# Sums of weights behind the low parts, another order of the first loads, and a shorter last 1/rms in a hybrid decoder

## The chip, the cores and the metric

The kernel runs on one core of one Trainium2 chip. The metric is the device time of one execution in microseconds (us). The core has five engines that each take their own queue of instructions in order: TensorE (PE, matrix products), VectorE (DVE), ScalarE (ACT), GpSimd (POOL) and SyncE (SP, which here issues the DMAs). They wait for one another through semaphores. PE's products land in PSUM, which has eight banks; the other engines read them from there.

## What is computed

A decoder of two layers on 512 tokens of 1024 features, float32. Each layer adds half of a SwiGLU network, then a mixer (gated linear attention in the first layer, stick-breaking attention in the second), then half of another network; an RMSNorm stands ahead of each and behind all:

```python
def rmsnorm(x, g):
    return x * lax.rsqrt(jnp.mean(x * x, axis=-1, keepdims=True) + EPS) * g

def swiglu(h, w_gate, w_up, w_down):          # 1024 -> 2816 -> 1024
    return (jax.nn.silu(h @ w_gate) * (h @ w_up)) @ w_down

for i in range(2):
    x = x + 0.5 * swiglu(rmsnorm(x, ffn1_norm[i]), ffn1_w_gate[i], ...)
    x = x + mixer_i(rmsnorm(x, mix_norm[i]))
    x = x + 0.5 * swiglu(rmsnorm(x, ffn2_norm[i]), ffn2_w_gate[i], ...)
return rmsnorm(x, final_norm)
```

## The kernel before, in words

The activations lie with features on the partitions: eight tiles of 128 features by 512 tokens (`x0` to `x7`). Weights come from memory in blocks of 1 MB (`raw`, gate and up, two buffers) and 512 KB (`rawd`, down, two buffers); SP issues these loads in its queue, and a load waits until the last reader of its buffer is done.

Full precision is had by splitting. ACT casts a block to a rounded high part (`wh`, line 126, in `Entry.split`), DVE subtracts it to get the low part (`wl`, line 127), and each product becomes three: high times high, low times high, high times low (`mm3`, line 68). The activations are split likewise (`nh`, `nl`; `hh`, `hl` by lines 788 and 789; `th`, `tl`).

The networks are computed in part by Strassen's scheme, with seven products of half blocks for eight. It needs sums and differences of the four quarters of a weight block: `s12` and `s34`, two DVE steps each, in `seven` at lines 677, 678, 683 and 684 (gate and up) and in `seven_down` at lines 353 to 361 (down). `Entry.view` (line 103) records these sums and `Entry.split` then cuts them like raw weights. `Feed.start` looks ahead: when a block's products begin, the next two entries are split, the next three viewed, the next five loaded. So a sum is recorded some blocks ahead of its product, at the point where its entry comes into view.

`seven` has two bodies. At the end of an up block stand these steps on what PE left in the banks: u3 from `ps_w` (line 736, ACT) and the sum with it (737, DVE); `ps_q` added into `o0` (740, DVE); the gate, a product of `o1` and `o0` each with the gate's part (707, DVE, in the shape `o<-o,o`); and the last quarter, `o1` from `ps_w` times the gate's part (707, DVE, in the shape `o<-ps_w,o`). Each reads a bank that a later product will use again: the banks go round in order of use. At three places in each network a down block follows at once, in `seven_down`: its first products are 12 into two new `ps_w` banks, 12 into two new `ps_q` banks (line 369), and then again 12 into the `ps_w` banks, which must first have been copied to `ps_z` by ACT (line 387). In the trace the tiles of `seven` are at line 694 and those of `seven_down` at 369.

The opening is written out by hand, with every instruction pinned in its order: `x` comes in halves of features, is turned by PE (line 1574), scaled by the norm's gain and split by ACT and DVE (1580, 1584), while squares for the norm are taken by ACT and DVE (1558, 1562); the first gate and up blocks are cut in halves (1544, 1546) and multiplied (1599). `keep` copies the turned tiles to `x0` to `x7` (1591, 1593).

At the end, `to_tokens` turns the activations back to tokens on partitions, and `last` (line 1458 and on) adds the last network's products to them in pieces, sums their squares (ACT, line 1471), takes 1/rms by `rstd_1` (495 to 506: a square root on ACT, a reciprocal and one Newton step on DVE), multiplies and writes out (1478 to 1481) by two DMAs on SP for each 128 tokens.

Of the kernel before, what the change touches and what calls it, by code (L numbers as in the profile page):

```python
# [10 lines left out]
F32 = mybir.dt.float32  # L11
# [21 lines left out]
def decoder(ctx: ExitStack, tc: tile.TileContext, a: dict, out: bass.AP):  # L33
    nc = tc.nc
# [59 lines left out]
    class Entry:  # L94
# [7 lines left out]

        def view(self):

            if self.views is None:
                self.views = [view(ch.load()) for ch, view, _, _ in self.units]
            return self.views

        def split(self):
            if self.W is None:  # L110
                self.W = []
                for r, (_, _, n, m) in zip(self.view(), self.units):
                    few = n * m < 1024
                    if few:

                        h = st["few"].tile([P, n * m + NEAR], F32R, tag="vh", bufs=1, name="wh")[:, NEAR:]
                        l = st["few"].tile([P, n * m + 64 - NEAR], F32R, tag="vl", bufs=1, name="wl")[:, : n * m]
                    else:
                        h, l = (
                            wp.tile([P, n * m + 64], F32R, tag="w" + t, bufs=4, name="w" + t)[  # L120
                                :, self.place : self.place + n * m
                            ]
                            for t in "hl"
                        )
                    h, l = (t.rearrange("p (n m) -> p n m", m=m) for t in (h, l))
                    st["cut"] = nc.scalar.copy(h, r).ins  # L126
                    nc.vector.tensor_tensor(out=l, in0=r, in1=h.bitcast(F32), op=ALU.subtract)  # L127
                    self.W.append((h, l))
                    if self.lead and len(self.W) == 1:


                        first = wp.tile([P, P], F32R, tag="w1", bufs=1, name="w1")
                        with tc.issue_after(st["cut"]):
                            nc.scalar.copy(first, r[:, 0, 0:P])
                        self.first = first
# [323 lines left out]
    st = {}  # L459
# [33 lines left out]

    def rstd_1(sums, more):

        v = sp.tile([P, 1], F32, tag="rv", bufs=2, name="rv")
        nc.vector.tensor_scalar(out=v, in0=sums, scalar1=more, scalar2=D * EPS, op0=ALU.add, op1=ALU.add)  # L497
        y = sp.tile([P, 1], F32, tag="ry", bufs=2, name="ry")
        nc.scalar.activation(y, v, AF.Sqrt)  # L499
        nc.vector.reciprocal(y, y)  # L500
        q = sp.tile([P, 1], F32, tag="rq", bufs=2, name="rq")
        nc.vector.scalar_tensor_tensor(out=q, in0=y, scalar=v, in1=y, op0=ALU.mult, op1=ALU.mult)  # L502
        c = float(D) ** 0.5
        nc.vector.tensor_scalar(out=q, in0=q, scalar1=-0.5 * c, scalar2=1.5 * c, op0=ALU.mult, op1=ALU.add)
        r = sp.tile([P, 1], F32, tag="r4", bufs=2, name="r1")
        nc.vector.tensor_tensor(out=r, in0=y, in1=q, op=ALU.mult)
        return r

    def rstd(sums, n):
# [932 lines left out]
    def to_tokens(tp):  # L1442
        st["tp"] = tp
        fin = st["fin"] = tp.tile([P, D], F32, tag="s", bufs=4, name="fin")
        nc.gpsimd.dma_start(fin, a["final_norm"].partition_broadcast(P))

        for hf in range(2):
            ps = [psum("ps_T") for _ in range(NT)]
            for m in range(4):
                for i in range(NT):  # L1450
                    nc.tensor.transpose(  # L1451
                        ps[i][:, m * P : (m + 1) * P], xs[hf * 4 + m][:, i * P : (i + 1) * P], ident
                    )
            for i in range(NT):
                xt[i, hf] = xs[hf * 4 + i]
                nc.scalar.copy(xt[i, hf], ps[i])

    def last(dh, i, ps, c0, c1):

        x, fin = xt[i, dh], st["fin"]  # L1460
        c = slice(c0, c1)
        nc.vector.scalar_tensor_tensor(out=x[:, c], in0=ps, scalar=0.5, in1=x[:, c], op0=ALU.mult, op1=ALU.add)  # L1462
        if c0 == 0:
            n = 2 * i + dh
        else:

            n = 2 * NT
            s = st["sq"][:, n - 2 : n - 1]
            nc.vector.tensor_tensor(out=s, in0=s, in1=st["sq"][:, n - 1 : n], op=ALU.add)
        sq = st["sq"][:, n : n + 1]  # L1470
        nc.scalar.activation(ps, x[:, c], AF.Square, accum_out=sq)  # L1471
        if dh == 0:
            st["xf"] = st["tp"].tile([P, T], F32, tag="s", bufs=4, name="xf")
            nc.vector.tensor_tensor(out=st["xf"], in0=x, in1=fin[:, 0:T], op=ALU.mult)
        elif c1 == T:
            rows = out[0, i * P : (i + 1) * P]
            r = rstd_1(sq, st["sq"][:, 2 * i : 2 * i + 1])
            nc.vector.scalar_tensor_tensor(out=x, in0=x, scalar=r, in1=fin[:, T:D], op0=ALU.mult, op1=ALU.mult)
            nc.sync.dma_start(rows[:, T:D], x)
            nc.scalar.activation(st["xf"], st["xf"], AF.Copy, scale=r)  # L1480
            nc.sync.dma_start(rows[:, 0:T], st["xf"])

    ffn(1, 0, 0, lambda k: prep(k, 2), first=True)
    phases.append(
# [9 lines left out]
    def begin(ip):  # L1494
# [22 lines left out]
        def load_x(hf):  # L1517
            for i in range(NT):
                x0[i, hf] = ip.tile([P, T], F32, name=f"x0_{i}_{hf}")
                nc.sync.dma_start(x0[i, hf], a["x"][0, i * P : (i + 1) * P, hf * T : (hf + 1) * T])  # L1520

        def load_w(e, hf):
            c = e.units[0][0]
            k = slice(hf * 4, hf * 4 + 4)
            nc.sync.dma_start(c.t[:, k], c.src[:, k])

        load_x(0), load_w(eg, 0), load_x(1), load_w(eu, 0), load_w(eg, 1), load_w(eu, 1)
        for c in phases[0].lead[2:]:
            nc.sync.dma_start(c.t, c.src)
        gains(1, ("mix_norm", "ffn2_norm", "gla_o_norm"))  # L1530
# [69 lines left out]


        psg = psum("ps_g")
        for i in range(NT):
            if i == 3:
                pin(nc.tensor.transpose(psg[:, 0:16], gls[0], ident[0:16, 0:16]))
            for k in range(4):
                turn(k, i)
        square(0, 0, True), square(1, 0, False), square(2, 0, True)
        pin(nc.vector.tensor_copy(gT[:, 0:16], psg[:, 0:16]))
        square(3, 0, False)  # L1610
        g, u = psum("ps_f"), psum("ps_f")
        scale(0)()
        cut(eg, 0)()
        square(0, 1, True), square(1, 1, False)
        scale(1)(), scale(2)()
        square(2, 1, True), square(3, 1, False)
        low = scale(3)

        n4 = lambda tag: sp.tile([P, NT], F32, tag=tag, bufs=2, name=tag)
        v, y, q, r4 = n4("rv"), n4("ry"), n4("rq"), n4("r4")  # L1620
# [8 lines left out]
                )  # L1629
            )  # L1630
        pin(nc.vector.tensor_scalar(out=v, in0=v, scalar1=1.0 / D, scalar2=EPS, op0=ALU.mult, op1=ALU.add))
        low()
        low = cut(eu, 0)
        st["sqrt"] = pin(nc.scalar.activation(y, v, AF.Sqrt)).ins
        keep(0), keep(1), keep(2)
        low()
        pin(nc.vector.reciprocal(y, y))
        pin(nc.vector.tensor_tensor(out=q, in0=y, in1=y, op=ALU.mult))
        pin(nc.vector.tensor_tensor(out=q, in0=q, in1=v, op=ALU.mult))
# [8 lines left out]
                )  # L1648
            )

        products(eg, g, (0, 1))
        for k in (4, 5):
            for i in range(NT):
                turn(k, i)
        products(eg, g, (2, 3))
        products(eu, u, (0, 1))
        for k in (6, 7):
            for i in range(NT):
                turn(k, i)
        products(eu, u, (2, 3))  # L1660
        ps = psum("ps_R")
        for i in range(NT):
            c = slice(i * P, (i + 1) * P)
# [74 lines left out]
```

## Time and profile before

| | |
|---|---|
| median of 3 runs | 1837.13 us (1836.43 to 1837.60) |
| the profiled execution's own time | 1839.01 us |
| its span, first to last instruction | 1837.2 us |
| granted TensorE clock, mean | 0.998 |
| PE / DVE / ACT busy in the span | 1821.0 / 1530.1 / 1068.4 us |
| DMA, mean | 98 GB/s |

Durations in the prediction come from the profiled execution, which took 1.9 us more than the median. A row of the timeline gives the start, the duration, the engine, the line, the operation and the tiles ("out<-in", buffer numbers left out); in brackets stands how long the engine was idle before it and what released it. Products are pipelined: a row is longer than the distance to the next row's start.

### The profile page before, as it was taken

What the parts mean: (1) busy time and instruction counts of PE and PEld (TensorE: products, weight loads), DVE (VectorE), ACT (ScalarE), POOL (GpSimd) and SP (SyncE); (2) the same over time, 40 slices, a digit from 0 to 9 for tenths busy, and PEclk for the clock granted to TensorE, in tenths of its full rate; (3) what the DMA queues carried; (4) which work ended last, traced back from release to release, by engine and by line L of the source; (5) the groups of instructions that cost most, each with busy time, mean ns of one, the idle gap of its engine ahead of it and who ended that gap; (6) DMA issues with size and microseconds to landing.
All of it is one profiled execution on the core that took longest, in us unless ns stands there. A gap on an engine that the chain in (4) does not pass through costs nothing. (4 is left out here: it accounts for less than half of the span.)

```text
span 1837.2 us, 30777 instructions
## 1 busy us (share of the span) xinstructions
PE 1821.0 (99%) x12476; PEld 1657.2 (90%) x12476; DVE 1530.1 (83%) x2509; ACT 1068.4 (58%) x1842; POOL 8.7 (0%) x20
## 2 busy tenths in 40 slices
PE   8999999999999999999999999999999999999998
PEld 7999999889888899999889999998888788999997
DVE  8999797776787989888798988976878769898885
ACT  6556565444555556555565555645878855565554
POOL 0000000100000000000000000000000000000000
PEclk9999999999999999999999999999999999999999
DMA  5333324221223232323233232322221222333331
GB/s 161 118 124 116 103 93 139 79 69 49 68 69 115 92 111 97 127 93 115 75 121 107 91 125 92 119 86 85 70 70 58 69 92 92 115 106 113 104 104 69
DMA packets 177649, 179.20 MB, mean 98 GB/s; under 512 B 4130, under 2 KB 168020, under 8 KB 177508
## 3 DMA queue, kind: packets, MB, share of 16 engines
q1 hardware_dynamic: 176800, 176.18, 30.2%
q8 instruction: 97, 1.59, 0.4%
q0 software_dynamic: 608, 1.05, 0.2%
q14 instruction: 44, 0.36, 0.1%
q10 hardware_dynamic: 100, 0.03, 0.0%
HBM read 175.17 MB, written 2.10 MB: 96 GB/s over the span
## 5 line engine op out<-in xcount | busy, mean ns | idle before, releaser
L127 DVE TENSOR_TENSOR wl<-raw,wh 128x1024 fp32r<-128x1024 f32 x242 | 256.0, 1061 | 88.0 <-ACT wh L126 46.6
L126 ACT CAST wh<-raw 128x1024 fp32r<-128x1024 f32 (+1 forms) x242 | 223.0, 922 | 157.4 <-PE ps_f L66 35.7
L127 DVE TENSOR_TENSOR wl<-s,wh 128x1024 fp32r<-128x1024 f32 x176 | 214.0, 1219 | 40.4 <-PE ps_z L694 38.5
L694 PE MATMUL ps_w<-th,wh 128*128 128x256 f32 x864 | 239.0, 277 | 0.3
L694 PE MATMUL ps_w<-tl,wh 128*128 128x256 f32 x864 | 238.7, 276 | 0.0
L694 PE MATMUL ps_w<-th,wl 128*128 128x256 f32 x864 | 238.7, 276 | 0.0
L126 ACT CAST wh<-s 128x1024 fp32r<-128x1024 f32 x176 | 184.9, 1050 | 82.8 <-DVE s L684 27.7
L66 PE MATMUL ps_f<-xh,wh 128*128 128x512 f32 x432 | 172.5, 399 | 0.0
L66 PE MATMUL ps_f<-xl,wh 128*128 128x512 f32 x432 | 169.3, 392 | 0.0
L66 PE MATMUL ps_f<-xh,wl 128*128 128x512 f32 x432 | 168.9, 391 | 0.0
L694 PEld LDWEIGHTS ps_w<-th,wh 128*128 128x128 f32 x864 | 162.2, 188 | 0.9 <-ACT ps_z L718 0.9
L694 PEld LDWEIGHTS ps_w<-th,wl 128*128 128x128 f32 x864 | 162.4, 188 | 0.0
L66 PE MATMUL ps_d<-hh,wl 128*128 128x512 f32 x416 | 162.2, 390 | 0.0
L66 PE MATMUL ps_d<-hh,wh 128*128 128x512 f32 x416 | 162.2, 390 | 0.0
L694 PEld LDWEIGHTS ps_w<-tl,wh 128*128 128x128 f32 x864 | 162.2, 188 | 0.0
L66 PE MATMUL ps_d<-hl,wh 128*128 128x512 f32 x416 | 161.8, 389 | 0.0
L126 ACT CAST wh<-rawd 128x1024 fp32r<-128x1024 f32 (+1 forms) x84 | 81.5, 971 | 96.7 <-PE ps_d L66 45.0
L127 DVE TENSOR_TENSOR wl<-rawd,wh 128x1024 fp32r<-128x1024 f32 (+1 forms) x84 | 93.2, 1118 | 20.7 <-PE ps_z L694 11.5
L324 DVE SCALAR_TENSOR_TENSOR x<-ps_d,x 128x512 f32<-128x512 f32 x120 | 80.9, 686 | 21.4 <-PE ps_d L66 21.0
L66 PEld LDWEIGHTS ps_f<-xl,wh 128*128 128x128 f32 x432 | 81.1, 188 | 17.3
L66 PEld LDWEIGHTS ps_f<-xh,wl 128*128 128x128 f32 x432 | 81.3, 188 | 15.6
L66 PEld LDWEIGHTS ps_f<-xh,wh 128*128 128x128 f32 x432 | 81.3, 188 | 15.4
(348 smaller groups left out, 5279.8 us busy)
## 6 DMA issues: line engine op xcount, KB each, us to landing
raw<-in_ffn_w_gate_dram SPq DMA_DIRECT2D x43, 1024.0 KB, 5.3
raw<-in_ffn_w_up_dram SPq DMA_DIRECT2D x43, 1024.0 KB, 5.7
rawd<-in_ffn_w_down_dram SPq DMA_DIRECT2D x84, 512.0 KB, 3.6
raw<-in_gla_w_in_dram SPq DMA_DIRECT2D x12, 1024.0 KB, 5.4
raw<-in_sb_w_in_dram SPq DMA_DIRECT2D x16, 512.0 KB, 3.8
raw<-in_gla_w_out_dram SPq DMA_DIRECT2D x4, 1024.0 KB, 5.0
raw<-in_sb_w_in_dram SPq DMA_DIRECT2D x4, 1024.0 KB, 5.2
raw<-in_sb_w_out_dram SPq DMA_DIRECT2D x4, 1024.0 KB, 5.0
```

The source lines that it names most:

```text
L66: st["pe"] = nc.tensor.matmul(ps, l, r, start=first, stop=last).ins
L126: st["cut"] = nc.scalar.copy(h, r).ins
L127: nc.vector.tensor_tensor(out=l, in0=r, in1=h.bitcast(F32), op=ALU.subtract)
L324: nc.vector.scalar_tensor_tensor(out=xs[k], in0=ps, scalar=0.5, in1=xs[k], op0=ALU.mult, op1=ALU.add)
L694: st["pe"] = nc.tensor.matmul(o, l_, r_, start=first and j + n == 0, stop=j == 3 and n == 2, skip_group_check=True).ins
```

## The change

Three edits, and what each does.

1. `Entry.view` records the sums of weights behind the last low part that was recorded before (`issue_after(st["low"])`); `split` keeps that low part in `st["low"]`.
2. In the opening, SP loads up's first half ahead of `x`'s second half. PE gets ten calls of a product of ones by ones of 128 columns: six ahead of the turning, one ahead of each of the last two tokens' tiles, two behind. Scaling, up's first cut and two copies go ahead of the squares of the second half; the products of the first four feature tiles with gate and with up stand together, and all turning of the second half behind them.
3. In the last 1/rms, the square root takes its bias on ACT, and a reciprocal, one combined step and a second reciprocal follow; the final gain is scaled ahead of time in `to_tokens`. For pieces behind the first, DVE takes the square; sums are kept running in `st["sum"]`. The last tile is multiplied and written in two halves on SP, and its other part is written from ACT's queue.

```diff
         def view(self):
             if self.views is None:
-                self.views = [view(ch.load()) for ch, view, _, _ in self.units]
+                with tc.issue_after(st["low"]) if "low" in st else ExitStack():
+                    self.views = [view(ch.load()) for ch, view, _, _ in self.units]
             return self.views
...
-                    nc.vector.tensor_tensor(out=l, in0=r, in1=h.bitcast(F32), op=ALU.subtract)
+                    st["low"] = nc.vector.tensor_tensor(out=l, in0=r, in1=h.bitcast(F32), op=ALU.subtract).ins
...
     def rstd_1(sums, more):
-        v = sp.tile([P, 1], F32, tag="rv", bufs=2, name="rv")
-        nc.vector.tensor_scalar(out=v, in0=sums, scalar1=more, scalar2=D * EPS, op0=ALU.add, op1=ALU.add)
         y = sp.tile([P, 1], F32, tag="ry", bufs=2, name="ry")
-        nc.scalar.activation(y, v, AF.Sqrt)
-        nc.vector.reciprocal(y, y)
-        q = sp.tile([P, 1], F32, tag="rq", bufs=2, name="rq")
-        nc.vector.scalar_tensor_tensor(out=q, in0=y, scalar=v, in1=y, op0=ALU.mult, op1=ALU.mult)
-        c = float(D) ** 0.5
-        nc.vector.tensor_scalar(out=q, in0=q, scalar1=-0.5 * c, scalar2=1.5 * c, op0=ALU.mult, op1=ALU.add)
+        nc.scalar.activation(y, sums, AF.Sqrt, bias=more)
+        v = sp.tile([P, 1], F32, tag="rq", bufs=2, name="rv")
+        nc.vector.tensor_tensor(out=v, in0=sums, in1=more, op=ALU.add)
         r = sp.tile([P, 1], F32, tag="r4", bufs=2, name="r1")
-        nc.vector.tensor_tensor(out=r, in0=y, in1=q, op=ALU.mult)
+        nc.vector.reciprocal(r, y)
+        nc.vector.scalar_tensor_tensor(out=v, in0=r, scalar=v, in1=y, op0=ALU.mult, op1=ALU.add)
+        nc.vector.reciprocal(r, v)
         return r
...
+        nc.vector.tensor_scalar(out=fin, in0=fin, scalar1=2.0 * float(D) ** 0.5, scalar2=None, op0=ALU.mult)
...
+        end = c0 > 0
+        if end:
+            junk = sp.tile([P, T], F32, tag="ss", name="junk")
+            nc.vector.scalar_tensor_tensor(
+                out=junk[:, 0 : c1 - c0], in0=x[:, c], scalar=1.0, in1=x[:, c], op0=ALU.mult, op1=ALU.mult, accum_out=sq
+            )
         else:
+            nc.scalar.activation(ps, x[:, c], AF.Square, accum_out=sq)
...
+            for a0, a1 in ((0, T // 2), (T // 2, T)) if end else ((0, T),):
+                nc.vector.scalar_tensor_tensor(
+                    out=x[:, a0:a1], in0=x[:, a0:a1], scalar=r, in1=fin[:, T + a0 : T + a1], op0=ALU.mult, op1=ALU.mult
+                )
+                nc.sync.dma_start(rows[:, T + a0 : T + a1], x[:, a0:a1])
             nc.scalar.activation(st["xf"], st["xf"], AF.Copy, scale=r)
-            nc.sync.dma_start(rows[:, 0:T], st["xf"])
+            (nc.scalar if end else nc.sync).dma_start(rows[:, 0:T], st["xf"])
...
-        load_x(0), load_w(eg, 0), load_x(1), load_w(eu, 0), load_w(eg, 1), load_w(eu, 1)
+        load_x(0), load_w(eg, 0), load_w(eu, 0), load_x(1), load_w(eg, 1), load_w(eu, 1)
...
+        def busy(n):
+            for _ in range(n):
+                pin(nc.tensor.matmul(u[:, 0:P], ones, ones, start=True, stop=True))
+        busy(6)
         for i in range(NT):
...
+            if i >= 2:
+                busy(1)
             for k in range(4):
                 turn(k, i)
+        busy(2)
...
         scale(0)()
         cut(eg, 0)()
+        scale(1)(), scale(2)(), scale(3)()
+        cut(eu, 0)()
+        keep(0), keep(1)
         square(0, 1, True), square(1, 1, False)
-        scale(1)(), scale(2)()
         square(2, 1, True), square(3, 1, False)
-        low = scale(3)
...
-        products(eg, g, (0, 1))
-        for k in (4, 5):
+        products(eg, g, range(4))
+        products(eu, u, range(4))
+        for k in range(4, KD):
             for i in range(NT):
                 turn(k, i)
-        products(eg, g, (2, 3))
-        products(eu, u, (0, 1))
-        for k in (6, 7):
-            for i in range(NT):
-                turn(k, i)
-        products(eu, u, (2, 3))
```

More of the change, by code (lines that the diff above doesn't have):

```diff
@@ L1462, in last @@
         nc.vector.scalar_tensor_tensor(out=x[:, c], in0=ps, scalar=0.5, in1=x[:, c], op0=ALU.mult, op1=ALU.add)
-        if c0 == 0:
-            n = 2 * i + dh
-        else:
[L1467 to L1471, printed above, removed]
+        end = c0 > 0
+        n = 2 * NT if end else 2 * i + dh
+        sq = st["sq"][:, n : n + 1]
+        if end:
[3 more added lines that the diff above has]
+            )
+        else:
+            nc.scalar.activation(ps, x[:, c], AF.Square, accum_out=sq)
         if dh == 0:
@@ L1474, in last @@
             nc.vector.tensor_tensor(out=st["xf"], in0=x, in1=fin[:, 0:T], op=ALU.mult)
-        elif c1 == T:
-            rows = out[0, i * P : (i + 1) * P]
-            r = rstd_1(sq, st["sq"][:, 2 * i : 2 * i + 1])
-            nc.vector.scalar_tensor_tensor(out=x, in0=x, scalar=r, in1=fin[:, T:D], op0=ALU.mult, op1=ALU.mult)
-            nc.sync.dma_start(rows[:, T:D], x)
+            st["sum"] = sp.tile([P, 1], F32, tag="rv", bufs=2, name="sum")
+            nc.vector.tensor_scalar(out=st["sum"], in0=sq, scalar1=D * EPS, scalar2=None, op0=ALU.add)
+        elif c1 < T:
+            nc.vector.tensor_tensor(out=st["sum"], in0=st["sum"], in1=sq, op=ALU.add)
+        else:
+            rows = out[0, i * P : (i + 1) * P]
+            r = rstd_1(sq, st["sum"])
+            for a0, a1 in ((0, T // 2), (T // 2, T)) if end else ((0, T),):
[3 more added lines that the diff above has]
+                nc.sync.dma_start(rows[:, T + a0 : T + a1], x[:, a0:a1])
             nc.scalar.activation(st["xf"], st["xf"], AF.Copy, scale=r)
-            nc.sync.dma_start(rows[:, 0:T], st["xf"])
+            (nc.scalar if end else nc.sync).dma_start(rows[:, 0:T], st["xf"])
     ffn(1, 0, 0, lambda k: prep(k, 2), first=True)
@@ L1602, in begin @@
         psg = psum("ps_g")
+        for k in range(4):
+            pst[k] = psum("ps_x")
+        g, u = psum("ps_f"), psum("ps_f")
+        def busy(n):
+            for _ in range(n):
+                pin(nc.tensor.matmul(u[:, 0:P], ones, ones, start=True, stop=True))
+        busy(6)
         for i in range(NT):
@@ L1610, in begin @@
         square(3, 0, False)
-        g, u = psum("ps_f"), psum("ps_f")
         scale(0)()
         cut(eg, 0)()
+        scale(1)(), scale(2)(), scale(3)()
+        cut(eu, 0)()
+        keep(0), keep(1)
         square(0, 1, True), square(1, 1, False)
-        scale(1)(), scale(2)()
         square(2, 1, True), square(3, 1, False)
-        low = scale(3)
         n4 = lambda tag: sp.tile([P, NT], F32, tag=tag, bufs=2, name=tag)
@@ L1631, in begin @@
         pin(nc.vector.tensor_scalar(out=v, in0=v, scalar1=1.0 / D, scalar2=EPS, op0=ALU.mult, op1=ALU.add))
-        low()
-        low = cut(eu, 0)
         st["sqrt"] = pin(nc.scalar.activation(y, v, AF.Sqrt)).ins
-        keep(0), keep(1), keep(2)
-        low()
+        keep(2)
         pin(nc.vector.reciprocal(y, y))
```

## The prediction

> **What bounds the kernel now.** I read the page's first part, then the view of TensorE's waits, then the timelines at the waits it names, because a kernel with a full engine can lose only where that engine stops.
>
> ```profile
> span 1837.2 us, 30777 instructions
> ...
> PE 1821.0 (99%) x12476; PEld 1657.2 (90%) x12476; DVE 1530.1 (83%) x2509; ACT 1068.4 (58%) x1842; POOL 8.7 (0%) x20
> ```
>
> TensorE (PE) is busy for 99% of the span, and the change takes no product away. So it can gain only in the opening, behind the last product, and in PE's few stops between. The largest of those, by the view of PE's waits (total, times, longest):
>
> ```profile
> PE ps_q L369 <- DVE o L707: 1.4, 1, 1.4
> PE ps_w L369 <- ACT ps_z L387: 1.2, 2, 0.7
> ```
>
> Both lines are in seven_down, the first products after an up block. The timeline shows the long one:
>
> ```profile
> 853.45 0.69 DVE L677 TENSOR_TENSOR s<-raw 128x512 f32<-128x512 f32 x1 [2.41 <-DMA raw<-in_ffn_w_up_dram]
> 854.06 0.42 DVE L740 TENSOR_TENSOR o<-ps_q,o 128x256 f32<-128x256 f32 x1
> ...
> 855.07 0.42 DVE L707 TENSOR_TENSOR o<-ps_w,o 128x256 f32<-128x256 f32 x1
> ```
>
> ```profile
> 853.83 0.28 PE L369 MATMUL ps_q<-hl,wh 128*128 128x256 f32 x1
> 855.54 0.38 PE L369 MATMUL ps_q<-hh,wh 128*128 128x256 f32 x1 [1.43 <-DVE o L707]
> ...
> 856.65 0.39 PE L369 MATMUL ps_w<-hh,wh 128*128 128x256 f32 x1
> ```
>
> VectorE (DVE) stands 2.41 us before a sum of weights whose block is still in flight; behind it in the queue stand the three steps that read PE's banks, and PE's next product needs one of these banks. A product starts 0.11 us after the one before, though its row is 0.28 long, so each stop is 0.17 longer from start to start than the view says: 1.6 here, 0.3 more before 856.65, and 1.2 + 2 x 0.17 = 1.5 for the two of the second line. Seven smaller stops, with no line of their own in the view, are 0.13 to 0.29 us beyond the step, 1.5 together; the first and the last of them:
>
> ```profile
> 168.48 0.28 PE L694 MATMUL ps_q<-tl,wh 128*128 128x256 f32 x1
> 168.88 0.38 PE L694 MATMUL ps_w<-th,wh 128*128 128x256 f32 x1
> ```
>
> ```profile
> 1659.23 0.28 PE L369 MATMUL ps_q<-hl,wh 128*128 128x256 f32 x1
> 1659.57 0.38 PE L369 MATMUL ps_q<-hh,wh 128*128 128x256 f32 x1
> ```
>
> One stop also costs clock. The windows view (length, PE, PEld, DVE, ACT, POOL busy, granted clock):
>
> ```profile
> 853.45:856.87 3.42, 1.85 (x13) 1.46 (x13) 3.42 (x7) 1.68 (x4) 0.00 (x0) 1.00 0.00 0
> 856.87:860.28 3.41, 3.41 (x18) 3.41 (x18) 2.95 (x7) 0.84 (x1) 0.00 (x0) 0.51 0.74 255
> 1040.59:1044.00 3.41, 2.72 (x24) 2.52 (x23) 3.41 (x7) 2.12 (x5) 0.00 (x0) 1.00 0.00 0
> ```
>
> PE idle for 1.57 of 3.42 us was followed by 3.41 us at half clock, in which 18 products ran that need 18 x 0.113 = 2.0: 1.4 us lost. Idle for 0.69 was followed by nothing. All these stops together: 1.6 + 0.3 + 1.5 + 1.5 + 1.4 = **6.3 us**.
>
> **The change part by part.** *Sums behind the low parts.* No sum stands any more between L737 and L740, where 23 of them stood. I followed the order of the built program's instructions: DVE takes L740's bank at once, and the two early steps behind it. So the 6.3 us of old stops go (between 4 and 6.3; the 1.4 of clock goes only if no stop there comes back). Weights do not come late by it: nearly all low parts are ready 4 to 9 us ahead of their product, and a sum pushed back by 1 to 4 us still is.
>
> What is late next: in the same order the third bank step, o<-ps_w (L706 after), has fallen back. At the end of an up block DVE now does o<-ps_q, the pair o<-o, a low part of 1024 columns, hl, a low part of 512, the first sum of the next block, and only then o<-ps_w. Before, o<-ps_w came right behind the pair. Whoever reuses that bank waits. The waits in the built program say who: of the 12 up blocks with a seven_down behind them, the second ps_q of seven_down waits on o<-ps_w at six (first network 1, second 2, third 1, fourth 2); at the others it waits on a step that is now early. One of the six, in rows of before:
>
> ```profile
> 703.37 0.69 DVE L677 TENSOR_TENSOR s<-raw 128x512 f32<-128x512 f32 x1
> 703.97 0.42 DVE L740 TENSOR_TENSOR o<-ps_q,o 128x256 f32<-128x256 f32 x1
> 704.31 0.75 DVE L707 TENSOR_TENSOR o<-o,o 128x256 f32<-128x256 f32 x2
> ...
> 705.31 1.22 DVE L127 TENSOR_TENSOR wl<-raw,wh 128x1024 fp32r<-128x1024 f32 x1
> 706.44 0.68 DVE L127 TENSOR_TENSOR wl<-rawd,wh 128x512 fp32r<-128x512 f32 x1
> 707.04 1.29 DVE L789 TENSOR_TENSOR hl<-o,hh 128x512 fp32r<-128x512 f32 x2
> ```
>
> ```profile
> 703.15 1.05 ACT L126 CAST wh<-raw 128x1024 fp32r<-128x1024 f32 x1 [0.93 <-PE ps_q L694]
> ```
>
> ```profile
> 706.35 0.28 PE L369 MATMUL ps_q<-hh,wh 128*128 128x256 f32 x1
> ```
>
> From start to start the steps are 0.34 (o<-ps_q), 0.67 (the pair), 1.13 (wl 1024), 0.60 (wl 512), 0.60 (hl), 0.60 (sum, 703.37 to 703.97). With the sum gone from the front, DVE takes o<-ps_q at 703.37 and reaches o<-ps_w at 703.37 + 0.34 + 0.67 + 1.13 + 0.60 + 0.60 + 0.60 = 707.31; its cast (703.15 + 1.05 = 704.20) doesn't hold it. It ends 0.42 later and PE starts 0.05 after that (855.07 + 0.42 to 855.54), at 707.78, where it started at 706.35: **1.43 us**. Four of the six have this sum ahead: **5.7 us**. Below that: nothing, if DVE had time in hand, which the rows exclude, since its first step waits for ACT's and PE's rows; above: 2.0 if the sum also waits for its block.
>
> The other two (the third place of the second and of the fourth network) have no sum ahead, but the low part of 1024 is that of a rawd block, and its load has moved. Before:
>
> ```profile
> 844.53 0.37 SPq L91 DMA_DIRECT2D rawd<-in_ffn_w_down_dram  x1
> 845.30 0.37 SPq L91 DMA_DIRECT2D raw<-in_ffn_w_up_dram  x1
> ```
>
> ```profile
> rawd<-in_ffn_w_down_dram SPq DMA_DIRECT2D x1, 512.0 KB, 3.3
> ```
>
> ```profile
> 850.74 1.05 ACT L126 CAST wh<-rawd 128x1024 fp32r<-128x1024 f32 x1 [0.93 <-PE ps_q L694]
> ```
>
> The rawd's buffer came free with a low part; now the four sums of the block in that buffer read it last (0.60 each), some 2 us later, and SP issues rawd behind raw. At 846.7, behind a 1 MB transfer, it lands at about 851.3 (at 850.0 if alone with 3.3 us; at 854 if raw again takes 8). ACT's cast of 850.74 then starts at 851.3, and DVE goes on 1.05 + 1.13 + 0.60 + 0.60 + 0.42 + 0.1 = 3.9 later, 855.2; PE wants it one step behind 853.83, at 853.94. So 1.26, or 0.7 with rawd in time, or 4 at the far end. For two places I take **2.0** (1.4 to 5). In the other networks the later rawd has slack: where rawd is cast first, the built order puts o<-ps_w of ACT 2.1 us behind it, still ahead of PE.
>
> *Clock after the new stops.* A stop of 1.43 is 1.26 idle in the view's measure, between 0.69 (no loss) and 1.57 (1.4 lost), nearer to the latter. It must lie in one stretch of 3.41 us, chance (3.41 - 1.43)/3.41 = 0.58, so 2.3 of four do; at even chances I take one half-clock stretch, **1.4 us** (none to six, 0 to 8.4).
>
> The Trainium skill, "TensorE: Matmul & The Clock Gate", Part 1, has the clock fall back after one idle window of about 3.4 us. By that rule no stop here would cost clock, and the sum would be 1.4 lower. This trace speaks against it: 1.57 us idle, with 13 products in the window, were enough.
>
> *Opening.* The products before 13.83 run at half speed:
>
> ```profile
> 11.51 0.63 PE L1599 MATMUL ps_f<-xh,wl 128*128 128x512 f32 x1
> 11.94 0.63 PE L1599 MATMUL ps_f<-xl,wh 128*128 128x512 f32 x1
> ...
> 14.66 0.39 PE L1599 MATMUL ps_f<-xh,wh 128*128 128x512 f32 x1
> 14.89 0.40 PE L1599 MATMUL ps_f<-xh,wl 128*128 128x512 f32 x1
> ```
>
> A step is 0.43 there and 0.23 later. Ten calls of ones products in the waits for x may lift the clock one or two stretches of 3.4 us earlier. Then six products save 0.2 each and eight transposes 0.1: 2.0 us, if PE set the pace; but DVE, with squares, low parts and copies, has hardly a gap from 9 to 24 us and keeps all its work. Bounds: -2.0, and +0.8 if the clock stays half and the four ones among and behind the transposes (two rows of 0.21 each) only stand in the way. I take **-1.0**. The earlier load of up's first half is hidden: x's second half is wanted later.
>
> *Tail.* After the last product nothing covers anything:
>
> ```profile
> 1830.31 0.42 DVE L1462 SCALAR_TENSOR_TENSOR x<-ps_bt,x 128x256 f32<-128x256 f32 x1 [0.31 <-PE ps_bt L66]
> ...
> 1830.83 0.39 ACT L1471 ACTIVATE ps_bt<-x 128x256 f32<-128x256 f32 x1 [0.23 <-DVE gT L1469]
> ...
> 1832.69 0.75 DVE L1478 SCALAR_TENSOR_TENSOR x<-x,r,fin 128x512 f32<-128x512 f32 x1
> ...
> 1833.48 0.33 SPq L1481 DMA_DIRECT2D out_dram<-xf  x1
> 1833.91 0.38 SPq L1479 DMA_DIRECT2D out_dram<-x  x1
> ```
>
> The square moves to DVE, right behind its own step (1830.65 for 1830.83), and of the small steps up to 1832.69 one goes: about 0.6 (0.4 to 0.8) earlier. The last multiply goes out in halves, and xf from ACT's own queue, so the last issue needn't stand behind another 0.43: **-1.0** together (-0.6 if the landing gives the second part back, -1.3 at best). The scaling of fin lies under the last products.
>
> **Sum.** -6.3 - 1.0 - 1.0 + 5.7 + 2.0 + 1.4 = +0.8 us. The profiled execution took 1839.01 (span 1837.2 and 1.8 around it), 1.9 over the median of 1837.13; I set the difference against the median: **1837.9 us**.
>
> **Rivals.** *The new stops cost only themselves* (no half clock at all): 1836.5. For it: idle of 0.69 cost nothing, and stops split by a boundary cost less. Against: 1.26 is nearer to 1.57. This is where that rule of the Trainium skill would lead.
>
> *Faster: the fallen-back step binds nowhere much.* If PE comes to these places later than now, or DVE earlier, the 7.7 us and their 1.4 of clock fall away: 1837.1 - 8.3 = 1828.8; with three of six binding some 1833. For it: waits are known from the built order, arrivals only from rows of before. Against: o<-ps_w can't run before ACT's cast of the same place, which PE itself releases.
>
> *Slower: half clock after each new stop.* Place: the same six; price 1.4 each, five more than I count, 7 us: 1844.9. It decides where the threshold lies below 1.26 idle, and more so if a rawd lands late and makes the third places longer than 2 us. For it: nearness to 1.57. Against: boundaries split four stops in ten.
>
> *The opening does not do what it says*: the ones leave the clock at half until 13.8. Then its -1.0 is between 0 and +0.8: 1838.9 to 1839.7.
>
> **How the numbers follow.** Forecast 0.33 (its own range 1834 to 1842), no half clock 0.12, faster 0.25, slower 0.24, opening idle 0.06. Two executions of this kernel can't be told apart below some 0.2% (3.7 us), so "same" is 1833.5 to 1840.8. Faster 0.25 comes from its rival; slower is its rival and 0.03 of the forecast, 0.27; the rest, 0.48, is same. The range leaves a tenth on each side: 1830 (inside the faster rival) to 1845 (the slower one's price).
>
> **What would show it.** Right: no DVE row of a sum with a DMA wait ahead of o<-ps_q; PE's waits in seven_down put down to DVE o L706, about six of 0.7 to 1.4; one or two stretches of granted clock near 0.5 in the middle; opening products at steps of 0.23 before 13.8; the last issue at about 1 us behind the last multiply. Wrong: PE's waits on L706 absent (then the faster rival), or half-clock rows behind most of them (the slower one), or waits of ACT's casts on rawd that hold PE for more than 2 us.

## The result, and the profile after

The changed kernel is slower, and outside the predicted range of 1830 to 1845 us.

| | before | after |
|---|---|---|
| median of 6 runs each | 1836.78 us (1834.62 to 1838.58) | 1850.32 us (1848.31 to 1854.70) |
| ratio of the times, 95% interval | | 1.0076 (1.0063 to 1.0089) |
| the profiled execution's own time | 1839.01 us | 1848.31 us |
| its span | 1837.2 us | 1846.5 us |

Before's profiled execution took longer than each of its six runs, and after's is the shortest of its six. So the two traces lie 9.3 us apart where the medians lie 13.5 apart: the traces show the places and the sizes, not all of the difference.

The first part of the page of after:

```profile
span 1846.5 us, 30844 instructions
...
PE 1822.9 (99%) x12496; PEld 1659.2 (90%) x12496; DVE 1538.9 (83%) x2513; ACT 1065.4 (58%) x1840; POOL 8.8 (0%) x20
```

PE is as full as before, and the ten calls of ones (two records each) are all that it has more. So the time went into its stops. PE's waits in after (total, times, longest):

```profile
PE ps_q L371 <- DVE o L706: 7.1, 6, 1.3
PE ps_w L371 <- DVE x L377: 5.6, 5, 1.3
PE ps_q L371 <- ACT o L703: 1.7, 1, 1.7
```

The first line is the one forecast, six waits on the step o<-ps_w. The second stood nowhere in the prediction: PE waits for the additions into x, by which DVE frees seven_down's banks. The third is a late load of rawd, once.

**A place of the first kind**, that of the prediction's rows. DVE's timeline in after:

```profile
706.92 0.42 DVE L739 TENSOR_TENSOR o<-ps_q,o 128x256 f32<-128x256 f32 x1
...
707.92 1.22 DVE L129 TENSOR_TENSOR wl<-raw,wh 128x1024 fp32r<-128x1024 f32 x1
709.05 0.68 DVE L788 TENSOR_TENSOR hl<-o,hh 128x512 fp32r<-128x512 f32 x1
...
710.26 0.68 DVE L676 TENSOR_TENSOR s<-raw 128x512 f32<-128x512 f32 x1
710.86 0.42 DVE L706 TENSOR_TENSOR o<-ps_w,o 128x256 f32<-128x256 f32 x1
```

PE's timeline at the same place:

```profile
709.78 0.28 PE L371 MATMUL ps_q<-hl,wh 128*128 128x256 f32 x1
711.33 0.38 PE L371 MATMUL ps_q<-hh,wh 128*128 128x256 f32 x1 [1.27 <-DVE o L706]
711.55 0.28 PE L371 MATMUL ps_q<-hh,wl 128*128 128x256 f32 x1
```

That is the order foretold, step by step, and the price: from 709.78 to 711.33 are 1.55 where a step is 0.11, a stop of 1.43 or 1.44 with the rounding of the rows, as forecast. The product that ends it takes 0.22 to the next start and not 0.11, so a stop costs 0.11 more than these 1.43.

**A place of the second kind**, 570 us earlier. DVE's timeline in before, then in after:

```profile
136.37 0.69 DVE L677 TENSOR_TENSOR s<-raw 128x512 f32<-128x512 f32 x1
...
140.04 1.29 DVE L789 TENSOR_TENSOR hl<-o,hh 128x512 fp32r<-128x512 f32 x2
...
141.92 0.74 DVE L375 SCALAR_TENSOR_TENSOR x<-ps_w,x 128x256 f32<-128x256 f32 x2
```

```profile
138.32 0.68 DVE L676 TENSOR_TENSOR s<-raw 128x512 f32<-128x512 f32 x1
138.93 0.41 DVE L706 TENSOR_TENSOR o<-ps_w,o 128x256 f32<-128x256 f32 x1
139.26 0.68 DVE L677 TENSOR_TENSOR s<-s,raw 128x512 f32<-128x512 f32 x1
139.86 0.68 DVE L682 TENSOR_TENSOR s<-raw 128x512 f32<-128x512 f32 x1
...
141.06 0.68 DVE L683 TENSOR_TENSOR s<-raw,s 128x512 f32<-128x512 f32 x1
...
142.33 0.74 DVE L377 SCALAR_TENSOR_TENSOR x<-ps_w,x 128x256 f32<-128x256 f32 x2
```

PE in before, and in after:

```profile
140.03 0.28 PE L369 MATMUL ps_w<-hh,wh 128*128 128x256 f32 x1
...
142.75 0.28 PE L369 MATMUL ps_w<-nh,wh 128*128 128x256 f32 x1
```

```profile
138.65 0.28 PE L371 MATMUL ps_w<-hh,wh 128*128 128x256 f32 x1
...
142.80 0.38 PE L371 MATMUL ps_w<-nh,wh 128*128 128x256 f32 x1 [1.27 <-DVE x L377]
```

Here o<-ps_w is in time. But all four sums of the next block now stand between the end of the up block and the additions into x; before, one of them stood ahead of o<-ps_q and three came behind the additions or earlier. PE is 1.38 earlier in after (138.65 for 140.03, the opening's gain), and the addition that frees ps_w is 0.41 later (142.33 for 141.92): against PE it has lost 1.79, three sums of 0.60. Before, it ended 0.36 ahead of its need (141.92 + 0.42 + 0.05 = 142.39 for 142.75). 1.79 - 0.36 = 1.43, the stop.

**All stops.** Each is the time from start to start beyond a usual step, without the 0.11 behind it. The six places forecast for o<-ps_w: four of 1.43 (at 257, 710, 1165 and 1627 us), 1.37 and 0.94 at the two third places: 8.0, where 7.7 was forecast. At the additions into x: 1.43 at 141, 832, 1048 and 1749 us and 0.70 at 291: 6.4. At the late rawd: 1.87. With two small ones 16.5 in all, against 5.0 in before: **11.5 us more**. No half clock follows any of them, so before's 1.4 of half clock is gone.

**Opening.** PE's timeline of after:

```profile
10.25 0.40 PE L1609 MATMUL ps_f<-xl,wh 128*128 128x512 f32 x1
10.49 0.40 PE L1609 MATMUL ps_f<-xh,wh 128*128 128x512 f32 x1
```

The step is 0.24 from 10.25 on, where it was 0.43 till 12.4. PE is ahead by 1.93 at 17 us, and keeps 1.4 of that (1.38 above, at 140 us).

**Tail.** The last product and the last issues in after:

```profile
1840.06 0.28 PE L66 MATMUL ps_bt<-wh,hl 128*128 128x256 f32 x1
...
1842.80 0.81 SPq L1489 DMA_DIRECT2D out_dram<-x  x2
1843.03 0.38 ACTq L1491 DMA_DIRECT2D out_dram<-xf  x1
```

From that product's start to the span's end are 1846.5 - 1840.06 = 6.4 us; before, 1837.2 - 1830.00 = 7.2: 0.8 gained.

**Account of the two traces.** -1.4 (opening) - 0.8 (tail) + 11.5 (stops) - 1.4 (half clock) + 2.0 (stretches in which PE's steps are some 4% longer, told in the last section) = +9.9, where the spans differ by 9.3.

### The profile page after: what moved, and what is told of

Read it like the earlier page. It is cut to its first block, busy times and chain, and to the rows that moved or that the text cites. A ratio compares the mean times of both kernels' runs of the same rounds, so it can differ in the third digit from the quotient of the medians.

```text
span 1846.5 us, 30844 instructions
## 1 busy us (share of the span) xinstructions
PE 1822.9 (99%) x12496; PEld 1659.2 (90%) x12496; DVE 1538.9 (83%) x2513; ACT 1065.4 (58%) x1840; POOL 8.8 (0%) x20
```

## The experiments

The theory at that point: the sums of gate's and up's weights, moved behind the low parts, load the short time in which DVE has to free banks at the start of seven_down; opening and tail gain little. The rival: the slowdown is mostly the opening's or the tail's doing, or a sum of many small things. Ratios are to the kernel before, on the same chip, with 95% intervals.

**One part at a time.** e1 is before with edit 1 alone; e2 is after without it; e3 and e4 are before with the opening or the tail alone.

```diff
e1, onto before
-                self.views = [view(ch.load()) for ch, view, _, _ in self.units]
+                with tc.issue_after(st["low"]) if "low" in st else ExitStack():
+                    self.views = [view(ch.load()) for ch, view, _, _ in self.units]
...
-                    nc.vector.tensor_tensor(out=l, in0=r, in1=h.bitcast(F32), op=ALU.subtract)
+                    st["low"] = nc.vector.tensor_tensor(out=l, in0=r, in1=h.bitcast(F32), op=ALU.subtract).ins
```

> The kernel before with the first edit alone: sums of weights recorded behind the last low part. Theory A (the sums now stand ahead of the steps by which DVE frees PE's banks, at all the places where seven_down follows an up block): slower than before by 13 to 16 us, the whole loss of the change and the 2 us that its other edits gain; PE stops of 1.43 us start to start at nine or ten places, and one near 1.9. Rival B (the loss comes from the other edits, or from how the edits lie together): within 3 us of before. The forecast on record would have +1.4 + 1.4 = about +3 us here.

> The changed kernel without its first edit: opening and last 1/rms as changed, sums where they were. Theory A: 1.5 to 2.5 us faster than before (opening about 1.4, tail about 0.8), PE's stops in the networks as before. Rival B: slower than before, or the same.

> The kernel before with the changed opening alone. From the trace of the changed kernel: the products of the first block start 1.4 us earlier at 37 to 53 us, so 1.0 to 1.6 us faster than before. Rival: the gain is taken back by a later wait of DVE for weights, so within 0.4 us.

> The kernel before with the changed last 1/rms, square on DVE and split writes alone. From the trace of the changed kernel: 0.77 us less behind the last product, so 0.5 to 1.0 us faster. Rival: the writes' landing takes it back, so within 0.3 us.

| | median us | before, same chip | ratio |
|---|---|---|---|
| e1 | 1849.15 | 1836.87 | 1.0066 (1.0053 to 1.0080) |
| e2 | 1836.42 | 1836.87 | 0.9996 (0.9987 to 1.0005) |
| e3 | 1836.86 | 1836.87 | 1.0003 (0.9994 to 1.0012) |
| e4 | 1837.34 | 1836.87 | 1.0003 (0.9994 to 1.0012) |

Edit 1 alone makes nearly all of the slowdown: 12.3 us, a little under the 13 to 16 expected. PE's waits in e1 (its own line numbers; the waits of the opening left out):

```profile
PE ps_q L370 <- DVE o L708: 5.9, 6, 1.3
PE ps_w L370 <- DVE x L376: 5.1, 4, 1.3
```

Both kinds are there, eight stops of 1.43, without the opening's faster start. The gains expected of the rest are not in the times: the interval of e2 leaves room for 2.4 us at most, those of e3 and e4 for 1.1. In e3's trace PE is 1.45 us ahead of before's until 130 us, and 0.6 behind at 300; between the two lie two stops of 0.3 at 256 us and a stretch of long steps (28 us from 266 on, 1.1 lost, see the last section) that before's trace doesn't have there. So the opening's gain is made, and is then lost among differences of its own size.

**Which sums.** e5 and e6 are e1 with the edit for gate's and up's sums only, or for down's only; e8 is after with the edit for down's only.

```diff
e6 (e5 has "and not any"; e8: the same in after)
-                with tc.issue_after(st["low"]) if "low" in st else ExitStack():
+                with tc.issue_after(st["low"]) if "low" in st and any(u[0].few for u in self.units) else ExitStack():
```

> The kernel before with the first edit for the sums of gate and up blocks alone (those of seven_down stay where they were). Theory A (four sums of 0.60 us now stand in DVE's queue between the end of an up block and the additions into x that free seven_down's banks, so DVE has more to do there than PE's products cover): 10 to 13 us slower than before, eight stops of 1.43. Rival C (the loss comes from the down blocks' sums, whose buffer comes free later, so that loads are late): within 2 us of before.

> The kernel before with the first edit for the sums of down blocks alone. In the built order no sum stands any more between the last ps_q step and the additions into x at most places, and o<-ps_w comes right behind its pair. Theory A: not slower, 0 to 4 us faster than before, no stop of 1.43, since the sum that waited for its load no longer stands ahead. Rival C: slower by 3 us or more, with stops put down to ACT's casts of rawd.

> The changed kernel with its first edit kept for the sums of down blocks alone. Theory A: as with the down sums alone and up to 2 us less for opening and tail: 1 to 5 us faster than before. Rival C: slower than before.

e5 took 1847.10 us, 1.0046 (1.0031 to 1.0060), with all eight stops of 1.43; its two lines of PE's waits are those of e1, number for number. It is 8.8 us slower than before, where 10 to 13 were expected.

e6 took 1839.70, 1.0008 (0.9999 to 1.0016), and has no stop of 1.43; three of 1.2 at other products (behind a seven_down, in products of gate or up; PE's waits below) and one of 1.5 on a late rawd bring its sum to 6.4:

```profile
PE ps_q L695 <- DVE x L376: 3.2, 4, 1.0
```

So the sums of gate and up are most of the cause: alone they make 0.46% of e1's 0.66%. Down's alone gain nothing, against the 0 to 4 us expected: the stops that they take away come back elsewhere. e8, expected 1 to 5 us faster than before, took 1843.99, 1.0028 (1.0017 to 1.0039), and that is Rival C's side. Its trace has 9.1 us of stops, one of 2.01 on a late rawd with half clock behind it, and 9 us lost in long steps; which of these the move of down's sums caused was not settled. The parts don't add up: down's sums and the rest, neither slower than before by more than 0.1% alone, are 0.28% slower together.

**Freeing the bank first.** e7 is after with every low part that is recorded behind the last o<-ps_w held behind it in DVE's order too.

```diff
-                    st["low"] = nc.vector.tensor_tensor(out=l, in0=r, in1=h.bitcast(F32), op=ALU.subtract).ins
+                    with tc.issue_after(st["gate"]) if "gate" in st else ExitStack():
+                        st["low"] = nc.vector.tensor_tensor(out=l, in0=r, in1=h.bitcast(F32), op=ALU.subtract).ins
...
-                    nc.vector.tensor_tensor(out=o[:, c : c + H], in0=t, in1=g[:, c : c + H], op=ALU.mult)
+                    m = nc.vector.tensor_tensor(out=o[:, c : c + H], in0=t, in1=g[:, c : c + H], op=ALU.mult)
+                    if c == 0 and o is v["o"][1]:
+                        st["gate"] = m.ins
```

> The changed kernel, with every low part recorded behind the last o<-ps_w step, so that this step comes right behind its pair and the low part of 1024 columns (1.13 us) falls behind the additions into x; the four sums stay ahead of those additions. Theory A (the amount of DVE work ahead of the additions counts, not the place of o<-ps_w): eight stops of 1.43 become about 0.3 each, at both kinds of place, so some 9 us faster than the changed kernel, 3 to 5 slower than before. Rival D, the mechanism of the forecast on record (only the place of o<-ps_w counts): the four stops at ps_q go, the four at ps_w of 1.43 stay: 6 us faster than the changed kernel.

1859.28 us, 1.0121 (1.0099 to 1.0143): worse than after. PE's waits in e7:

```profile
PE ps_q L694 <- DVE x L378: 9.3, 4, 2.3
PE ps_w L372 <- DVE x L378: 7.6, 12, 0.9
```

The waits on o<-ps_w are gone, and the additions into x hold PE for 0.7 to 1.1 us at all twelve places. Four stops of 2.50 and three of 1.52 stand some 10 us behind the up block's end, where neither theory had one. DVE's timeline shows why:

```profile
263.88 1.22 DVE L130 TENSOR_TENSOR wl<-raw,wh 128x1024 fp32r<-128x1024 f32 x1
265.01 2.36 DVE L130 TENSOR_TENSOR wl<-s,wh 128x1024 fp32r<-128x1024 f32 x2
...
275.49 1.23 DVE L130 TENSOR_TENSOR wl<-s,wh 128x1024 fp32r<-128x1024 f32 x1 [1.79 <-PE ps_z L694]
```

The low part that gave way joins two others, and with sums between them the next additions into x come late. Then DVE stands idle for 1.79, waiting for PE. The work isn't too much for DVE; it stands in the wrong place, and a move of one step pushes the queue to the next one.

**One step more at the place.** If DVE runs without a gap into these stops, one step more there costs its full 0.60; if DVE had time left, nothing. e9 (after) and e10 (before) get a reduction of 512 columns ahead of the additions in each seven_down; its value goes into no result.

```diff
+    fill = cp.tile([P, 1], F32, name="fill")
...
+            with tc.issue_after(st["gate"]):
+                one = gT[:, 50:51].to_broadcast([P, T])
+                nc.vector.tensor_reduce(out=fill, in_=one, axis=mybir.AxisListType.X, op=ALU.add)
...
(and st["gate"] as in e7)
```

> The changed kernel with one more VectorE step of about 0.6 us (a reduction whose result nobody reads) in each seven_down, right ahead of the additions into x that free its banks; the rest of the order as in the changed kernel. Theory A (at the places with a stop of 1.43, DVE has no time left ahead of these additions): at each of the eight places PE stops for 0.6 us more in all, 4 to 6 us slower than the changed kernel. Rival E (the stops are set by the weights' casts or loads, and DVE waits there too): within 1.5 us of the changed kernel, the stops still 1.43.

> The kernel before with the same extra step right ahead of its additions into x. Theory A: in the order of before these places have some 0.5 to 1 us to spare, so no new stop over 0.5 us and less than 2.5 us slower. If the places had nothing to spare before either, the same 4 to 6 us as in the changed kernel.

e9: 1860.21 us, 1.0119 (1.0105 to 1.0133) against after's 1.0076, some 8 us more where 4 to 6 were expected. The place of the second kind, in PE's timeline:

```profile
143.66 0.39 PE L372 MATMUL ps_w<-nh,wh 128*128 128x256 f32 x1 [1.87 <-DVE x L378]
```

The wait of 1.27 has become 1.87: the step's full 0.60, so DVE has no time left there. Behind the stops of the first kind a new one of 0.47 stands each time. The stops' sum is 23.5, 7 more than in after; three stretches of half clock come on top.

e10: 1844.44, 1.0034 (1.0021 to 1.0046), 6.3 us slower than before where less than 2.5 was expected. It doesn't answer its question, since the built order changed by more than the step. At the place of the second kind, DVE's timeline:

```profile
141.48 1.22 DVE L128 TENSOR_TENSOR wl<-raw,wh 128x1024 fp32r<-128x1024 f32 x1
```

In before this low part of 1.13 stood ahead of the additions (at 138.31). Now it stands behind the first three of them, PE has no stop there, and four stops of 0.8 to 0.9 stand at others of these places, some 10 us behind the up block's end, as in e7. What before has in hand is shown by its own rows alone, 0.36 at that place.

**The sums on another engine.** e11 (after) and e12 (before) have GpSimd (POOL) do the four sums of gate's and up's blocks.

```diff
-                nc.vector.tensor_tensor(out=s[:, 0:4], in0=t[:, 0:4, P:], in1=t[:, 4:8, P:], op=ALU.add)
+                nc.gpsimd.tensor_tensor(out=s[:, 0:4], in0=t[:, 0:4, P:], in1=t[:, 4:8, P:], op=ALU.add)
...
(and the three others alike)
```

> The changed kernel with the four sums of each gate and up block on GpSimd, which is idle in the networks; the down blocks' sums stay on VectorE behind the low parts. Theory A: with the sums out of DVE's queue the eight stops of 1.43 go or fall to some 0.8 (o<-ps_w still stands behind one low part and two short steps), so 5 to 11 us faster than the changed kernel. Against it: how long a sum takes on GpSimd is not shown yet; if over about 2.5 us each, ACT's casts wait for them and PE stops there.

> The kernel before with the four sums of each gate and up block on GpSimd. Theory A, with sums of up to 2.5 us: DVE never stands before a load for a sum, its stops go: 0 to 4 us faster than before. If sums on GpSimd are slow or slow DVE down: slower than before, stops put down to ACT's casts or to DVE.

1991.01 us, 1.0832 (1.0814 to 1.0850), and 1923.80, 1.0469 (1.0451 to 1.0487). Groups of e12, by shape (busy us, mean ns of one):

```profile
L683 POOL TENSOR_TENSOR s<-raw 128x512 f32<-128x512 f32 x72 | 130.6, 1814 | 72.4 <-DVE wl L127 47.7 <-DVE tl L789 23.4 <-DVE nl L789 1.3
...
L737 DVE TENSOR_TENSOR o<-u,o 128x256 f32<-128x256 f32 x72 | 53.2, 738 | 0.1
L740 DVE TENSOR_TENSOR o<-ps_q,o 128x256 f32<-128x256 f32 x72 | 29.9, 415 | 1.7 <-PE ps_q L694 1.7
```

And the same groups of before:

```profile
L683 DVE TENSOR_TENSOR s<-raw 128x512 f32<-128x512 f32 x72 | 49.3, 684 | 0.0
...
L737 DVE TENSOR_TENSOR o<-u,o 128x256 f32<-128x256 f32 x72 | 30.2, 419 | 0.0
L740 DVE TENSOR_TENSOR o<-ps_q,o 128x256 f32<-128x256 f32 x72 | 30.1, 418 | 0.0
```

This sum takes 2.7 times as long on POOL beside a busy DVE, and DVE's step with both inputs in SBUF grows from 419 to 738 ns beside it, while the one that reads a PSUM bank stays at 415. So this doesn't relieve DVE, and both kernels are far slower though a sum stays under the 2.5 us that the expectations allowed. The Trainium skill, "SBUF — State Buffer", section "SBUF: two separate sides", says that VectorE steps with two SBUF inputs and GpSimd steps that read SBUF lock each other out of a shared pair of ports; these two rows agree.

**Sums viewed one block later.** e13 (after) and e14 (before) look three entries ahead in place of four, so each sum is recorded one block later.

```diff
-            for e in self.q[i : i + 4]:
+            for e in self.q[i : i + 3]:
```

> The changed kernel, with sums recorded one block later (three entries ahead instead of four). By the built order DVE then has, between the last ps_q step and the first addition into x of seven_down, one low part of 1024, one of 512, o<-ps_w, two hl and one sum: 1.13 + 0.33 + 4 x 0.60 = 3.9 us, where the changed kernel has 5.7 (four sums) and the kernel before 3.3 (none). Theory A (this amount decides; 5.7 gives a stop of 1.43): no stop of 1.43 at these places, so 8 us or more faster than the changed kernel, within 4 us of before. If instead the edge behind the low parts as such costs, or casts that come later, it stays 8 us or more slower than before.

> The kernel before, with sums recorded one block later and no edge behind the low parts. At the places after an up block the built order is the one of before (3.3 us). Theory A: no stop of 1.43, within 4 us of before; how far below it depends on whether the stops behind a load go, since the loads then have one block more to land: 0 to 4 us faster if so. If the later sums make casts late: slower, stops put down to ACT's casts.

e13 took 1863.15, 1.0133 (1.0117 to 1.0149), where 8 us faster than after was expected. Its largest wait of PE:

```profile
PE ps_q L693 <- DVE x L377: 9.0, 4, 2.3
```

The two lines of after, L706 and L377 at L371, have shrunk from 7.1 and 5.6 to 1.6 and 1.4, so that much of the expectation held. The stops stand at later products instead, longer, as in e7. The casts on ACT now wait for sums that DVE hasn't done. In after, then in e13, of all waits:

```profile
ACT wh L128 <- DVE s L683: 70.0, 31, 7.6
```

```profile
ACT wh L128 <- DVE s L683: 112.6, 64, 7.4
```

e14 took 1841.92, 1.0019 (1.0008 to 1.0030). With no move behind the low parts, three entries ahead leave the networks only 3.1 us of stops, no half clock and no stop of 1.43, and yet it is 4.6 us slower: its trace has 285 us of long steps, told below, at a loss of 10.7, where before has 105 at 3.9.

## Why the prediction was wrong, point by point

1. *The old stops go*: right in mechanism. No sum waits for its block ahead of o<-ps_q any more, and the half clock went with the long stop. Their price, 6.3, was that of one execution: e2, e3 and e4 leave the networks' order as it was before, and their traces have 3.5, 4.4 and 2.9 us of stops and no half clock there.
2. *Six places at which o<-ps_w is late, four at 1.43 and 2.0 for the two third places*: right in place, mechanism and size, 8.0 for 7.7. e1 and e5 show the four of 1.43 without the rest of the change; the third places take 0.58 each there, near the 0.7 that the prediction gave for a rawd in time.
3. *"At the others it waits on a step that is now early"*: **the step that failed.** It is true of the second ps_q, and the second ps_q is only the first product that could wait. The same four sums also stand ahead of the additions into x, which free the banks of the products that follow, and there the sum should have been worked out too. It would have come from rows like those that were at hand: three sums more ahead of the addition, 3 x 0.60 = 1.8, less 0.36 in hand, 1.43. Four places of that and one of 0.70 make **6.4 us** that the prediction gave to nobody. e9 shows that DVE has no gap at these four places.
4. *rawd cast first, "still ahead of PE"*: wrong once. ACT's timeline of after:

```profile
1083.43 1.05 ACT L128 CAST wh<-rawd 128x1024 fp32r<-128x1024 f32 x1 [1.54 <-DMA rawd<-in_ffn_w_down_dram]
...
1085.20 0.37 ACT L703 ACTIVATE o<-ps_w 128x256 f32<-128x256 f32 x1
```

   The cast waits 1.54 for rawd, o<-ps_w of ACT behind it ends at 1085.57, and PE stops for 1.87. Slack of 2.1 in the order was no slack in time. SP issued this rawd at 1078.72, as soon as the last of down's sums had read its buffer, and in before at 1073.03; raw, released by a low part, went from 1073.64 to 1075.39. So against raw the rawd was 3.9 us later, where the prediction had some 2. e6, with down's sums alone, has the same stop (1.54).
5. *Half clock after the new stops, +1.4*: none came, in this execution, and the rival without it was right. By the stretches of the last section a stop of 1.43 alone is too short: it left 19 products or more in its 3.41 us, and 15 were enough to keep the clock. Three stretches in e9, two in e13 and one in e8 show half clock behind stops of about 2 us and more.
6. *Opening -1.0*: -1.4 in the traces; *tail -1.0*: -0.8. Both right in sign, and in the medians of e2, e3 and e4 neither shows.
7. Not in the sum at all: long steps, 2.0 between these two traces.

As a difference: +0.8 (forecast) + 8.3 (points 3 and 4) - 1.4 (half clock that did not come) + 2.0 (long steps) = +9.7, where the spans of the two profiled executions differ by 9.3. The medians differ by 13.5; the 4.2 beyond are the distance of the two profiled executions from their medians: before's is 2.2 above, after's 2.0 below. No trace of an execution nearer to the medians shows where these lie.

The rival that ends on the slower side put its 1844.9 on half clock. It had the sign, and not the mechanism.

## What to carry to other kernels

When a step moves back in an in-order queue, work out every later step of that queue against the engine that waits for it, until a gap in the queue has taken up the delay; the first waiter is one of several. An idle wait that work used to fill isn't gained when the work leaves it: here the sums left a place where DVE had to wait for PE anyhow (at 703 us, ahead of the place of the first kind, DVE idles 1.3 us where it idled 0.6), and stood at one where PE waited for DVE. And a later place for one step of such a queue, as in e7 and e13, moves the wait to the next bank rather than away. Before's longest stop hung on a load, and no trace of e2, e3 or e4 has it at that place, though their networks have before's order: one trace doesn't price such a stop.

## What the runs showed of the hardware

*Steps that are 4% longer at full granted clock.* PE's timeline of after, in two stretches without a wait:

```profile
1149.77 0.28 PE L693 MATMUL ps_w<-th,wh 128*128 128x256 f32 x1
...
1150.90 0.28 PE L693 MATMUL ps_w<-th,wl 128*128 128x256 f32 x1
...
1169.77 0.28 PE L371 MATMUL ps_z<-hh,wh 128*128 128x256 f32 x1
...
1170.95 0.28 PE L371 MATMUL ps_w<-t,wl 128*128 128x256 f32 x1
```

Ten steps take 1.13 us in the first and 1.18 in the second. In after such stretches of 8 to 38 us lie at 258, 448, 860, 1167 and 1777 us, four of the five starting within 2 us behind a stop; the granted clock is shown as 1.00 in them. Together with shorter ones they last 105 us in before (3.9 lost), 160 in after (5.9), 67 in e7 (2.4) and 285 in e14 (10.7). e7 has the longest stops and the least of them, e14 the shortest and the most, so the stops alone don't explain them. What does stays open; they are one reason why two kernels whose stops differ by 2 us can't be told apart.

*Half clock goes by fixed stretches of 3.41 us, not by the length of a stop.* In each trace the half-clock stretches start and end on a grid of 3.413 us that begins where the opening's half clock ends: in before at 13.84, and 856.93 and 860.34 lie 247 and 248 steps behind it; in e9 at 4.20, and its six edges in the networks lie 41, 42, 308, 309, 319 and 320 steps behind. One stretch of this grid and the next, in e7 and then in e8 (busy PE and its products first, granted clock after POOL):

```profile
1761.71:1765.12 3.41, 1.61 (x15) 1.41 (x13) 3.31 (x8) 0.98 (x2) 0.00 (x0) 1.00 0.11 19
1765.12:1768.53 3.41, 2.88 (x25) 2.88 (x26) 3.15 (x6) 0.37 (x1) 0.00 (x0) 1.00 0.86 289
```

```profile
1081.80:1085.21 3.41, 1.56 (x13) 1.36 (x12) 1.91 (x4) 2.95 (x7) 0.00 (x0) 1.00 0.01 2
1085.21:1088.62 3.41, 3.41 (x19) 3.41 (x17) 2.00 (x4) 0.04 (x1) 0.00 (x0) 0.50 0.84 280
```

e7's stop is 2.50 us long and keeps the clock, since an edge of the grid cuts it; e8's of 2.01 lies whole in one stretch and loses it. A stretch has room for 30 products of 256 columns (3.413 / 0.113). In the networks of all kernels but e11 and e12, the seven stretches with 14 products or fewer (before 14, e8 13, e9 14, 13 and 13, e13 12 and 10) were each followed by half clock, and none with 15 or more was (the fewest: 15 twice in e7, twice in e9 and once in e3). After's late rawd has 17, its stops of 1.43 leave 19 or more. So in these traces a stop costs clock only if it takes more than about 2.0 us out of one stretch, and where the edges lie differs from trace to trace. The rule weighed in the prediction (the Trainium skill, "TensorE: Matmul & The Clock Gate", Part 1: one whole idle window) disagrees: stretches that were partly busy were enough. The same part of the Trainium skill has the window run freely, without a reset at the kernel's start; these edges agree.
